# Log-sum-exp over rows on one core: rows split 112 plus 16 instead of 120 plus 8, a smaller final store, and the rarely used second pass placed in front of the first in the program

## Chip, core, metric

One core of a Trainium2 chip runs the kernel alone. The metric is device time in microseconds (us), the median of several executions. The profile's span leaves out some 1.8 us that the time has besides (163.79 against 162.0 in the profiled run of before).

## The reference

```python
x = randn(32, 512, 1024)                        # float32, 67.1 MB
max_x = max(x, axis=-1)
out = max_x + log(sum(exp(x - max_x), axis=-1)) # 16384 results
```

## The kernel before

The 16384 rows lie on 128 partitions, 128 rows each. The first pass does without the maximum: it takes Exp, sums, and Ln, and counts whether any sum is out of range. Only if one is, a second pass, with the maximum, overwrites the result. For inputs like these it never runs, but its code is in the program.

Rows come in 17 groups through a ring of 48 rows per partition. `R5` is one Exp of 5 rows on ScalarE and one reduction on VectorE; `T3` is an Exp and then for each row a half-add with accumulation on VectorE; `A` is one row that ScalarE both exponentiates and sums. Each load goes out on SyncE's queue and leaves sixteen updates of its semaphore in the records; those of the last load came from 157.57 to 158.13 us, and the Exp that needs it started at 158.16.

```python
B = 8; W = NC - B                  # NC = 128 rows per partition
x_rows = x_flat[0 : P * W].rearrange("(p c) d -> p c d", p=P)
x_rest = x_flat[P * W : n].rearrange("(p c) d -> p c d", p=P)
loads = ["R8 R8", "R8 R8", "R8 R8", "R7 R6 A A", "R6 R5 A A A", "R5 R4 A", "R5 R4", "R5 T3",
         "R3 A A A", "R3 A", "R2 T2", "R3", "R1 A", "T2", "T1", "A", "A"]
REST = 7; EARLY = 104; LATE = 118
for i, ops in enumerate(loads):    # the eighth group comes from x_rest, columns 0 to 7
    ...                            # load, Exp, sums
    if following == EARLY + 14:
        nc.scalar.activation(out=res[:, 0:EARLY], in_=sumexp[:, 0:EARLY], func=AF.Ln)
    if following == LATE + 3:
        check(0, LATE, 0)          # range check of the sums on VectorE
nc.at_finalize(start_early)        # SyncE's first load goes to the top, before the opening barrier
nc.scalar.activation(out=res[:, EARLY:NC], in_=sumexp[:, EARLY:NC], func=AF.Ln)
nc.sync.dma_start(out=out_rest, in_=res[:, 0:B])     # 32 bytes a partition
nc.sync.dma_start(out=out_rows, in_=res[:, B:NC])    # 480 bytes a partition, the last to land
... # range check of the rest, flag to ScalarE and VectorE
with tc.If(all_fine < 1, preferred_fallthrough_block=False):
    ... # second pass, in steps of 48 rows
```

The order in which instructions stand on an engine is not the source's: a scheduler in the build decides it. In this kernel the source has the early Ln after the eleventh group (118 rows); in the trace below it ran at 141.67 us, in front of the Exps of groups ten and eleven.

Of the kernel before, what the change touches and what calls it, by code (L numbers as in the profile page):

```python
# [14 lines left out]
def kernel(  # L15
# [5 lines left out]
    nc = tc.nc  # L21
# [3 lines left out]
    AF = mybir.ActivationFunctionType  # L25
# [6 lines left out]
    NC = n // P  # L32
# [2 lines left out]



    B = 8
    W = NC - B
    x_rows = x_flat[0 : P * W].rearrange("(p c) d -> p c d", p=P)  # L40
    x_rest = x_flat[P * W : n].rearrange("(p c) d -> p c d", p=P)
    out_flat = out.rearrange("a b -> (a b)")
    out_rows = out_flat[0 : P * W].rearrange("(p c) -> p c", p=P)
    out_rest = out_flat[P * W : n].rearrange("(p c) -> p c", p=P)
# [3 lines left out]

    RING = 48
    loads = [  # L50
        "R8 R8", "R8 R8", "R8 R8", "R7 R6 A A", "R6 R5 A A A", "R5 R4 A", "R5 R4", "R5 T3",
        "R3 A A A", "R3 A", "R2 T2", "R3", "R1 A", "T2", "T1", "A", "A",
    ]
    loads = [[(op[0], int(op[1:] or 1)) for op in load.split()] for load in loads]
    assert sum(s for ops in loads for _, s in ops) == NC
    ENGINES = [mybir.EngineType.Activation, mybir.EngineType.DVE]
    REST = 7
    EARLY = 104
    LATE = 118
    LAST = NC - 1  # L60

    big = ctx.enter_context(tc.tile_pool(name="big", bufs=1))
# [3 lines left out]
    ring = big.tile([P, RING, d], fp32, name="ring")  # L66
    sumexp = stats.tile([P, NC], fp32, name="sumexp")
    res = stats.tile([P, NC], fp32, name="res")
# [10 lines left out]
    nc.vector.memset(far, 100 * HIGH)  # L79

    def source(c0, size):
        assert c0 >= B or (c0 == 0 and size == B)
        return x_rows[:, c0 - B : c0 - B + size, :] if c0 >= B else x_rest

    def load(p0, c0, size, i):


        step = {2: 4, 3: 2, 4: 2}.get(i, 1)
        return [
            nc.sync.dma_start(  # L90
                out=ring[k::step, p0 : p0 + size, :], in_=source(c0, size)[k::step]
            ).ins
            for k in range(step)
        ]
# [14 lines left out]
        )  # L109
        nc.tensor.matmul(count, lhsT=bad[:, i : i + 1], rhs=far, start=i == 0, stop=False)  # L110

    following = B
    p = 0
    for i, ops in enumerate(loads):
        size = sum(s for _, s in ops)
        if p + size > RING:
            p = 0
        if i == REST:
            c = 0
        else:  # L120
            c = following
            following += size
        dmas = load(p, c, size, i)
        if i == 0:
            first_load = dmas[0]
        for how, s in ops:
            v = ring[:, p : p + s, :]
            sums = sumexp[:, c : c + s]
            if how == "A":
                o = v if c < LAST else last_exp  # L130
                exp = nc.scalar.activation(out=o, in_=v, func=AF.Exp, accum_out=sums)  # L131
            else:
                exp = nc.scalar.activation(out=v, in_=v, func=AF.Exp)  # L133
            without_wait(exp, "loads", "the slot's earlier users came before this load")
            without_wait(exp, "exps", "the slot's earlier users came before this load")
            without_wait(exp, "sums", "the slot's earlier users came before this load")
            tc.add_to_no_dep_group("exps", exp.ins)
            added = []
            if how == "R":
                added = [nc.vector.reduce_sum(out=sums, in_=v, axis=AX.X)]  # L140
            elif how == "T":
                for r in range(s):
                    lo = ring[:, p + r, 0:H]
                    added.append(
                        nc.vector.scalar_tensor_tensor(  # L145
                            out=lo, in0=lo, scalar=1.0, in1=ring[:, p + r, H:d],
                            op0=ALU.mult, op1=ALU.add, accum_out=sums[:, r : r + 1],
                        )
                    )
            for add in added:  # L150
                for dma in dmas:
                    tc.declare_no_dep(add.ins, dma, reason="ScalarE has waited for it")
                without_wait(add, "loads", "they came before this one")
            for add in added:
                tc.add_to_no_dep_group("sums", add.ins)
            c += s
            p += s
            last_row = v
        for dma in dmas:
            tc.add_to_no_dep_group("loads", dma)  # L160
        if following == EARLY + 14:
            nc.scalar.activation(out=res[:, 0:EARLY], in_=sumexp[:, 0:EARLY], func=AF.Ln)  # L162
        if following == LATE + 3:
            check(0, LATE, 0)

    def start_early(program):

        blocks = program.main_func.blocks
        here = next(b for b in blocks if any(i.name == first_load.name for i in b.instructions))
        k = next(k for k, i in enumerate(here.instructions) if i.name == first_load.name)  # L170
        assert not here.instructions[k].has_wait()
        first = here.instructions.pop(k)
        top = blocks[0].instructions
        k = next(
            k for k, i in enumerate(top)
            if i.engine == mybir.EngineType.SP and isinstance(i, mybir.InstDrain)
        )
        top.insert(k, first)

    nc.at_finalize(start_early)  # L180

    nc.scalar.activation(out=res[:, EARLY:NC], in_=sumexp[:, EARLY:NC], func=AF.Ln)  # L182
    nc.sync.dma_start(out=out_rest, in_=res[:, 0:B])
    nc.sync.dma_start(out=out_rows, in_=res[:, B:NC])



    check(LATE, LAST, 1)
    nc.vector.reduce_max(out=bad[:, 3:4], in_=last_row[:, 0, 0 : d // 16], axis=AX.X)  # L189
    nc.vector.tensor_scalar(  # L190
        out=bad[:, 2:3], in0=bad[:, 3:4], scalar1=LOG_LOW, scalar2=None, op0=ALU.is_lt
    )
    nc.tensor.matmul(count, lhsT=bad[:, 2:3], rhs=far, start=False, stop=False)  # L193
    nc.tensor.matmul(count, lhsT=sumexp[:, LAST:NC], rhs=ones, start=False, stop=True)  # L194
    nc.vector.tensor_scalar(out=fine, in0=count, scalar1=HIGH, scalar2=None, op0=ALU.is_lt)  # L195
# [4 lines left out]
    with tc.If(all_fine < 1, preferred_fallthrough_block=False):  # L200
        with tc.tile_critical(sync_engine=mybir.EngineType.Activation):
            with nc.semaphore("landed") as landed, nc.semaphore("ready") as ready:
                rows = 0
                steps = 0
                for c0 in range(0, NC, RING):
                    s = min(RING, NC - c0)
                    v = ring[:, 0:s, :]
                    neg = clamped[:, c0 : c0 + s]
                    if c0:
                        nc.scalar.wait_ge(ready, steps)  # L210
                    for c1, s1 in ((0, B), (B, s - B)) if c0 == 0 else ((c0, s),):
                        nc.scalar.dma_start(
                            out=ring[:, c1 - c0 : c1 - c0 + s1, :], in_=source(c1, s1)
                        ).then_inc(landed, 16)
                        rows += 16
                    nc.vector.wait_ge(landed, rows)
                    nc.vector.tensor_reduce(
                        out=neg, in_=v, op=ALU.max, axis=AX.X, negate=True
                    ).then_inc(ready, 1)
                    nc.vector.wait_ge(ready, steps + 1)  # L220
                    nc.vector.tensor_add(
                        out=v, in0=v, in1=neg[:, :, None].to_broadcast([P, s, d])
                    ).then_inc(ready, 1)
                    nc.scalar.wait_ge(ready, steps + 2)
                    nc.scalar.activation(out=v, in_=v, func=AF.Exp).then_inc(ready, 1)
                    nc.vector.wait_ge(ready, steps + 3)
                    nc.vector.reduce_sum(
                        out=sumexp[:, c0 : c0 + s], in_=v, axis=AX.X
                    ).then_inc(ready, 1)
                    steps += 4  # L230
                nc.scalar.wait_ge(ready, steps)
                nc.scalar.activation(out=res, in_=sumexp, func=AF.Ln).then_inc(ready, 1)
                nc.vector.wait_ge(ready, steps + 1)
                nc.vector.tensor_sub(out=res, in0=res, in1=clamped).then_inc(ready, 1)
                nc.scalar.wait_ge(ready, steps + 2)
                nc.scalar.dma_start(out=out_rest, in_=res[:, 0:B]).then_inc(landed, 16)
                nc.scalar.dma_start(out=out_rows, in_=res[:, B:NC]).then_inc(landed, 16)
                nc.scalar.wait_ge(landed, rows + 32)


# [28 lines left out]
```

## Time and profile before

| | before |
|---|---|
| time, median | 163.84 us (163.82 to 163.94) |
| loads, first packet to last | 1.02 to 157.69 us, 428 GB/s |
| last row landed / its Exp starts | 158.13 / 158.16 us |
| early Ln: ScalarE reaches it / its sums are ready | 141.67 / 140.41 us |
| final store, issue to landing | 159.58 to 161.16 us |

The page gives busy shares, the windows view what moved in a stretch, the timeline when each instruction ran, with its idle time in brackets where there was some. The lines that carry these readings are in the prediction. Here is the timeline of ScalarE in the kernel before, around the Ln and up to the end (start, length, engine, line, what):

```profile
141.58 0.19 ACT L131 ACTIVATION_READ_ACCUMULATOR ring<-ring 128x1 f32 x1
141.67 0.27 ACT L162 ACTIVATE res<-sumexp 128x104 f32<-128x104 f32 x1
141.85 2.75 ACT L133 ACTIVATE ring<-ring 128x3072 f32<-128x3072 f32 x1
...
154.35 2.86 ACT L133 ACTIVATE ring<-ring 128x2048 f32<-128x2048 f32 x2 [0.24 <-DMA ring<-in_x_dram]
```

The Ln has no bracket: it ran at once. The only idle time behind it that the view reports is 0.24 us before the Exp at 154.35. ScalarE has almost no room in its last 17 us.

### The profile page before, as it was taken

What the parts mean: (1) busy time and instruction counts of PE and PEld (TensorE: products, weight loads), DVE (VectorE), ACT (ScalarE), POOL (GpSimd) and SP (SyncE); (2) the same over time, 40 slices, a digit from 0 to 9 for tenths busy, and PEclk for the clock granted to TensorE, in tenths of its full rate; (3) what the DMA queues carried; (4) which work ended last, traced back from release to release, by engine and by line L of the source; (5) the groups of instructions that cost most, each with busy time, mean ns of one, the idle gap of its engine ahead of it and who ended that gap; (6) DMA issues with size and microseconds to landing.
All of it is one profiled execution on the core that took longest, in us unless ns stands there. A gap on an engine that the chain in (4) does not pass through costs nothing.

```text
span 162.0 us, 216 instructions
## 1 busy us (share of the span) xinstructions
PE 0.6 (0%) x8; PEld 0.3 (0%) x8; DVE 122.4 (76%) x47; ACT 116.8 (72%) x53; POOL 0.2 (0%) x4
## 2 busy tenths in 40 slices
PE   0000000000000000000000000000000000000001
PEld 0000000000000000000000000000000000000000
DVE  0000000899949999499999995999998999979993
ACT  3000059980799609994599839999969599999993
POOL 0000000000000000000000000000000000000000
DMA  8995995996996999799999899899999999999980
GB/s 275 502 518 259 518 518 259 518 518 275 502 518 291 485 502 425 303 485 485 453 453 453 382 394 425 384 453 437 437 396 469 394 455 401 425 423 417 414 350 19
DMA packets 2818, 67.19 MB, mean 415 GB/s; under 512 B 640, under 2 KB 640, under 8 KB 1024
## 3 DMA queue, kind: packets, MB, share of 16 engines
q1 hardware_dynamic: 2816, 67.18, 97.0%
q14 instruction: 2, 0.02, 0.0%
HBM read 67.11 MB, written 0.07 MB: 415 GB/s over the span
## 4 chain that ended last, share of the span: by engine, by line
DMA 63%; DVE 22%; ACT 12%; issue 0%; SPq 0%; PE 0%; DVEq 0%; ACTq 0%
DMA ring<-in_x_dram 63%; DVE sumexp L140 21%; ACT ring L133 12%; DVE ring L145 1%; SPq L90 0%; PE count L193 0%; DVE clamped L102 0%; DVE bad L190 0%; DVE bad L189 0%; DVE clamped L106 0%; DVE fine L195 0%; PE count L194 0%; DVEq L102 0%; ACTq L133 0%
## 5 line engine op out<-in xcount | busy, mean ns | idle before, releaser
L140 DVE TENSOR_REDUCE sumexp<-ring 128x8 f32<-128x8192 f32 (+7 forms) x20 | 116.2, 5854 | 36.0 <-ACT ring L133 36.0
L133 ACT ACTIVATE ring<-ring 128x8192 f32<-128x8192 f32 (+7 forms) x24 | 101.7, 4283 | 42.0 <-DMA ring<-in_x_dram 41.9
L131 ACT ACTIVATE ring<-ring 128x1024 f32<-128x1024 f32 x12 | 12.5, 1040 | 0.0
L145 DVE SCALAR_TENSOR_TENSOR ring<-ring 128x512 f32<-128x512 f32 x8 | 5.1, 683 | 0.0
L131 ACT ACTIVATION_READ_ACCUMULATOR ring<-ring 128x1 f32 x12 | 2.2, 186 | 0.0
L77 ACT ACT_TABLE_LOAD x1 | 1.3, 1283 | 0.8 <-PEq L253 0.8
L131 ACT ACTIVATE last_exp<-ring 128x1024 f32<-128x1024 f32 x1 | 1.0, 1028 | 0.0
L110 PE MATMUL count<-far,bad 128*1 128x1 f32 x4 | 0.4, 164 | 158.8 <-DVE clamped L106 158.8
L78 DVE MEMSET ones<- 128x1 f32 x1 | 0.1, 59 | 0.9 <-PEq L253 0.9
L145 DVE DVE_READ_ACCUMULATOR ring<-ring 128x1 f32 x8 | 0.6, 81 | 0.0
L102 DVE TENSOR_SCALAR clamped<-sumexp 128x118 f32<-128x118 f32 (+1 forms) x2 | 0.4, 198 | 0.1
L106 DVE SCALAR_TENSOR_TENSOR clamped<-clamped,sumexp 128x118 f32<-128x118 f32 (+1 forms) x2 | 0.4, 224 | 0.1
L110 PEld LDWEIGHTS count<-far,bad 128*1 128x1 f32 x4 | 0.2, 80 | 158.9 <-DVE clamped L106 158.9
L195 DVE TENSOR_SCALAR fine<-count 1x1 int32<-1x1 f32 x1 | 0.1, 145 | 0.3 <-PE count L194 0.3
L162 ACT ACTIVATE res<-sumexp 128x104 f32<-128x104 f32 x1 | 0.3, 272 | 0.0
L182 ACT ACTIVATE res<-sumexp 128x24 f32<-128x24 f32 x1 | 0.2, 222 | 0.0
L189 DVE TENSOR_REDUCE bad<-ring 128x1 f32<-128x64 f32 x1 | 0.2, 219 | 0.0
L193 PE MATMUL count<-far,bad 128*1 128x1 f32 x2 | 0.2, 164 | 0.2 <-DVE bad L190 0.2
L194 PE MATMUL count<-ones,sumexp 128*1 128x1 f32 x2 | 0.2, 163 | 0.0
L131 ACT ACTIVATION_READ_ACCUMULATOR last_exp<-ring 128x1 f32 x1 | 0.2, 186 | 0.0
L190 DVE TENSOR_SCALAR bad<-bad 128x1 f32<-128x1 f32 x1 | 0.2, 153 | 0.0
L106 DVE DVE_READ_ACCUMULATOR clamped<-clamped,sumexp 128x1 f32 x2 | 0.2, 82 | 0.0
(7 smaller groups left out, 0.6 us busy)
## 6 DMA issues: line engine op xcount, KB each, us to landing
ring<-in_x_dram SPq DMA_DIRECT2D x2, 3840.0 KB, 27.7
ring<-in_x_dram SPq DMA_DIRECT2D x2, 3584.0 KB, 25.6
ring<-in_x_dram SPq DMA_DIRECT2D x1, 5120.0 KB, 31.3
ring<-in_x_dram SPq DMA_DIRECT2D x1, 4608.0 KB, 33.7
ring<-in_x_dram SPq DMA_DIRECT2D x1, 4096.0 KB, 29.3
ring<-in_x_dram SPq DMA_DIRECT2D x2, 2048.0 KB, 32.7
ring<-in_x_dram SPq DMA_DIRECT2D x1, 3072.0 KB, 36.2
ring<-in_x_dram SPq DMA_DIRECT2D x2, 1024.0 KB, 38.7
```

The costliest lines, as they stand in the source:

```text
L77: nc.scalar.preload_act_table_set("natural_log_exp_and_others")
L102: nc.vector.tensor_scalar(out=clamped[:, c0:c1], in0=sumexp[:, c0:c1], scalar1=LOW, scalar2=HIGH, op0=ALU.max, op1=ALU.min,)
L106: nc.vector.scalar_tensor_tensor(out=clamped[:, c0:c1], in0=clamped[:, c0:c1], scalar=0.0, in1=sumexp[:, c0:c1], op0=ALU.bypass, op1=ALU.n ...
L110: nc.tensor.matmul(count, lhsT=bad[:, i : i + 1], rhs=far, start=i == 0, stop=False)
L131: exp = nc.scalar.activation(out=o, in_=v, func=AF.Exp, accum_out=sums)
L133: exp = nc.scalar.activation(out=v, in_=v, func=AF.Exp)
L140: added = [nc.vector.reduce_sum(out=sums, in_=v, axis=AX.X)]
L145: nc.vector.scalar_tensor_tensor(out=lo, in0=lo, scalar=1.0, in1=ring[:, p + r, H:d], op0=ALU.mult, op1=ALU.add, accum_out=sums[:, r : r + 1],
L162: nc.scalar.activation(out=res[:, 0:EARLY], in_=sumexp[:, 0:EARLY], func=AF.Ln)
L182: nc.scalar.activation(out=res[:, EARLY:NC], in_=sumexp[:, EARLY:NC], func=AF.Ln)
L189: nc.vector.reduce_max(out=bad[:, 3:4], in_=last_row[:, 0, 0 : d // 16], axis=AX.X)
L190: nc.vector.tensor_scalar(out=bad[:, 2:3], in0=bad[:, 3:4], scalar1=LOG_LOW, scalar2=None, op0=ALU.is_lt)
```

## The change

The intent, as the diff tells: let the last store carry little (64 bytes a partition instead of 480), put the large one among the loads, and take the jump over the second pass out of the end of the program, where it costs (gaps of 0.36 us on ScalarE and 0.52 us on VectorE), to the very top, where both have little to do anyway (in the kernel before the first Exp starts at 22.04 us, the first reduction at 29.10). The early Ln stays after 118 rows in the source, but takes 112 columns instead of 104.

```diff
-    B = 8
+    B = 16
     loads = [
-        "R8 R8", "R8 R8", "R8 R8", "R7 R6 A A", "R6 R5 A A A", "R5 R4 A", "R5 R4", "R5 T3",
-        "R3 A A A", "R3 A", "R2 T2", "R3", "R1 A", "T2", "T1", "A", "A",
+        "R8 R8", "R8 R8", "R6 R5 R5", "R8 R8", "R6 R5 A A A A", "R4 R4 R4", "R7 A A", "R4 T3",
+        "R4 A", "T2 A", "R2 A", "T2 A", "T2", "T2", "T1", "A", "A",
     ]
-        if following == EARLY + 14:
-            nc.scalar.activation(out=res[:, 0:EARLY], in_=sumexp[:, 0:EARLY], func=AF.Ln)
-        if following == LATE + 3:
+        if c == LATE:
+            nc.scalar.activation(out=res[:, 0:W], in_=sumexp[:, 0:W], func=AF.Ln)
             check(0, LATE, 0)
 ...
+        barrier = [...]                     # the opening barrier of ScalarE and VectorE
+        here.instructions[0:0] = barrier    # now behind their jump
+        for b in [b for b in blocks if "_true" in b.name or "critical" in b.name]:
+            blocks.remove(b)
+            blocks.insert(blocks.index(here), b)    # second pass in front of the first
 ...
-    nc.scalar.activation(out=res[:, EARLY:NC], in_=sumexp[:, EARLY:NC], func=AF.Ln)
-    nc.sync.dma_start(out=out_rest, in_=res[:, 0:B])
-    nc.sync.dma_start(out=out_rows, in_=res[:, B:NC])
+    nc.scalar.activation(out=res[:, W:NC], in_=sumexp[:, W:NC], func=AF.Ln)
+    nc.sync.dma_start(out=out_rows, in_=res[:, 0:W])
+    nc.sync.dma_start(out=out_rest, in_=res[:, W:NC])
 ...
-                for c0 in range(0, NC, RING):
+                for c0 in range(0, NC, STEP):       # STEP = 6: a longer second pass
```

More of the change, by code (lines that the diff above doesn't have):

```diff
@@ L56 @@
     ENGINES = [mybir.EngineType.Activation, mybir.EngineType.DVE]
-    REST = 7
-    EARLY = 104
     LATE = 118
+    STEP = 6
     LAST = NC - 1
@@ L81, in source @@
     def source(c0, size):
-        assert c0 >= B or (c0 == 0 and size == B)
-        return x_rows[:, c0 - B : c0 - B + size, :] if c0 >= B else x_rest
+        assert c0 >= W or c0 + size <= W
+        return x_rest[:, c0 - W : c0 - W + size, :] if c0 >= W else x_rows[:, c0 : c0 + size, :]
     def load(p0, c0, size, i):
@@ L110, in check @@
         nc.tensor.matmul(count, lhsT=bad[:, i : i + 1], rhs=far, start=i == 0, stop=False)
-    following = B
+    c = 0
     p = 0
@@ L117 @@
             p = 0
-        if i == REST:
-            c = 0
-        else:
-            c = following
-            following += size
         dmas = load(p, c, size, i)
@@ L160, with arrange @@
             tc.add_to_no_dep_group("loads", dma)
-        if following == EARLY + 14:
-            nc.scalar.activation(out=res[:, 0:EARLY], in_=sumexp[:, 0:EARLY], func=AF.Ln)
-        if following == LATE + 3:
+        if c == LATE:
+            nc.scalar.activation(out=res[:, 0:W], in_=sumexp[:, 0:W], func=AF.Ln)
             check(0, LATE, 0)
-    def start_early(program):
+    def arrange(program):
         blocks = program.main_func.blocks
+        top = blocks[0].instructions
         here = next(b for b in blocks if any(i.name == first_load.name for i in b.instructions))
@@ L172, in start_early @@
         first = here.instructions.pop(k)
-        top = blocks[0].instructions
         k = next(
@@ L178, in start_early @@
         top.insert(k, first)
-    nc.at_finalize(start_early)
-    nc.scalar.activation(out=res[:, EARLY:NC], in_=sumexp[:, EARLY:NC], func=AF.Ln)
-    nc.sync.dma_start(out=out_rest, in_=res[:, 0:B])
-    nc.sync.dma_start(out=out_rows, in_=res[:, B:NC])
+        barrier = [
+            i for i in top
+            if i.engine in ENGINES and isinstance(i, (mybir.InstDrain, mybir.InstEventSemaphore))
+        ]
+        assert len(barrier) == 2 * len(ENGINES)
+        for i in barrier:
+            top.remove(i)
+        here.instructions[0:0] = barrier
+        for b in [b for b in blocks if "_true" in b.name or "critical" in b.name]:
+            blocks.remove(b)
+            blocks.insert(blocks.index(here), b)
+    nc.at_finalize(arrange)
+    nc.scalar.activation(out=res[:, W:NC], in_=sumexp[:, W:NC], func=AF.Ln)
+    nc.sync.dma_start(out=out_rows, in_=res[:, 0:W])
+    nc.sync.dma_start(out=out_rest, in_=res[:, W:NC])
     check(LATE, LAST, 1)
@@ L204 @@
                 steps = 0
-                for c0 in range(0, NC, RING):
-                    s = min(RING, NC - c0)
+                for c0 in range(0, NC, STEP):
+                    s = min(STEP, NC - c0)
                     v = ring[:, 0:s, :]
@@ L210 @@
                         nc.scalar.wait_ge(ready, steps)
-                    for c1, s1 in ((0, B), (B, s - B)) if c0 == 0 else ((c0, s),):
+                    edge = max(c0, min(W, c0 + s))
+                    for c1, c2 in ((c0, edge), (edge, c0 + s)):
+                        if c1 == c2:
+                            continue
                         nc.scalar.dma_start(
-                            out=ring[:, c1 - c0 : c1 - c0 + s1, :], in_=source(c1, s1)
+                            out=ring[:, c1 - c0 : c2 - c0, :], in_=source(c1, c2 - c1)
                         ).then_inc(landed, 16)
@@ L235 @@
                 nc.scalar.wait_ge(ready, steps + 2)
-                nc.scalar.dma_start(out=out_rest, in_=res[:, 0:B]).then_inc(landed, 16)
-                nc.scalar.dma_start(out=out_rows, in_=res[:, B:NC]).then_inc(landed, 16)
+                nc.scalar.dma_start(out=out_rest, in_=res[:, W:NC]).then_inc(landed, 16)
+                nc.scalar.dma_start(out=out_rows, in_=res[:, 0:W]).then_inc(landed, 16)
                 nc.scalar.wait_ge(landed, rows + 32)
```

## The prediction

> **What bounds the kernel now.** I read the page first: the busy line, then the slices, then the DMA queues.
>
> ```profile
> PE 0.6 (0%) x8; PEld 0.3 (0%) x8; DVE 122.4 (76%) x47; ACT 116.8 (72%) x53; POOL 0.2 (0%) x4
> ...
> q1 hardware_dynamic: 2816, 67.18, 97.0%
> q14 instruction: 2, 0.02, 0.0%
> HBM read 67.11 MB, written 0.07 MB: 415 GB/s over the span
> ```
>
> No compute engine is above 76%, while the load queue alone fills 97.0% of the time of 16 DMA engines. Next, the windows view of the load stretch and of the tail; its last two columns are the DMA share and GB/s.
>
> ```profile
> 1.00:158.00 157.00, 0.19 (x2) 0.09 (x2) 121.00 (x38) 115.02 (x49) 0.00 (x0) 1.00 1.00 427
> 158.00:162.00 4.00, 0.43 (x6) 0.22 (x6) 1.27 (x8) 1.53 (x5) 0.00 (x0) 1.00 0.07 19
> ```
>
> So the time has three pieces: 1.0 us until the first packet (packet records: 1.02 us), a stream without a gap from there to 157.69 us (67.11 MB in 156.67 us, 428 GB/s), and a tail of 4.3 us. After the span of 162.0 come 1.8 us more, since that run took 163.79. Only three things can save time: an earlier start, fewer bytes or less packet overhead, a shorter tail.
>
> The tail, in the timeline (start, length, engine, line):
>
> ```profile
> 157.11 1.04 ACT L131 ACTIVATE ring<-ring 128x1024 f32<-128x1024 f32 x1
> ...
> 158.16 1.03 ACT L131 ACTIVATE last_exp<-ring 128x1024 f32<-128x1024 f32 x1
> ...
> 159.12 0.19 ACT L131 ACTIVATION_READ_ACCUMULATOR last_exp<-ring 128x1 f32 x1
> ...
> 159.34 0.22 ACT L182 ACTIVATE res<-sumexp 128x24 f32<-128x24 f32 x1
> ...
> 159.58 0.34 SPq L184 DMA_DIRECT2D out_dram<-res  x1
> 159.64 0.14 DVE L195 TENSOR_SCALAR fine<-count 1x1 int32<-1x1 f32 x1 [0.33 <-PE count L194]
> ```
>
> The last row lands at 158.13 (its semaphore's sixteenth update), its Exp starts at 158.155, then accumulator, Ln, store at 159.58. The store's packets run from 160.42 to 160.77 and it lands at 161.16. Meanwhile ScalarE and VectorE load the flag and branch over the second pass. Who is waited for at the end, from the queue's waits within 156 to 162 us:
>
> ```profile
> SPq L264 <- DVEq L200: 0.5, 1, 0.5
> SPq L264 <- DMA out_dram<-res: 0.3, 1, 0.3
> SPq L264 <- ACTq L200: 0.3, 1, 0.3
> ```
>
> The sequencers' records give the order of arrival at the closing barrier: ScalarE's drain ends at 161.06, VectorE's at 161.25, SyncE's second drain (after the store landed) at 161.31, and the gather passes at 161.33. So SyncE and the store set the end, but VectorE is only 0.05 us behind as a second path. Its branch is slow: the jump's record starts at 160.63 and lasts 0.05, and the next record, the drain, starts at 161.20, a gap of 0.52 us. ScalarE has a gap of 0.36 us after its compare (160.37 to 160.73). [...] The two packets of the instruction queue, 8192 bytes each, start at 161.39 and 161.79, about 0.95 us after each of these gaps opens[...].
>
> [...]
>
> **The change part by part.**
>
> *Load list.* Still 17 groups and 128 rows per partition, and 22 load DMAs in the same partition splits. Between landings I read 19.345 us for 16 rows in one group and about 1.277 for one row: 15 rows are 18.07, so a row costs 1.2045 and a group some 0.07 beyond. 128 rows and 17 groups in both kernels: zero. Does the queue run dry? I stepped both lists through ring, engines and queue group by group, with the durations of this trace (Exp 0.85 us a row, reduction 1.08, half-add row 0.61). For before, this gives issues within 0.8 us of those traced (46.4, 65.8, 76.6, 85.2 us). For after, the tightest point is the group of nine rows: it must wait for the second reduction of the fourth group, about 104 us, and the queue still has some 7 us of bytes. No gap.
>
> *Tail of the load list.* The last rows arrive in groups of 2, 1, 1, 1 as before. The row sums put into half-adds (12 instead of 8 rows) and one row less on the accumulating Exp move VectorE's end of row sums from 158.47 to about 158.1, but ScalarE's last Exp waits for the last landing (158.13) anyway: zero on the path.
>
> *Stores.* The large one (now 112 columns, 448 bytes a partition) goes out after group eleven, about 147 to 149 us. It stands behind every load in the queue, as the old 32-byte one did (its packets ran 157.12 to 157.74), so it delays no load and lands by about 158.5, long before the end. The final one shrinks from 480 to 64 bytes a partition. Packets of 480 bytes took 26.4 ns, 32-byte ones 9.0; eight a DMA engine are 0.21 us; at an estimated 10 ns they are 0.08. Saved: 0.13. The Ln before it has 16 instead of 24 columns: from 104 columns (272 ns) against 24 (222) 0.6 ns a column, 0.005. The store path gets about 0.14 us shorter[...].
>
> *Code placement.* The jump at the very top costs VectorE and ScalarE perhaps half a microsecond there, and the opening barrier, which now comes after it, waits. SyncE's first load is issued before the barrier and fills the queue for 19 us, and the first Exp starts at 22.04: free. At the end the second pass is no longer in the way: [...]VectorE's drain comes at about 160.75 instead of 161.20. Alone that saves nothing, because the store lands later. Together with the small store it keeps VectorE from taking over: the store alone would gain only 0.05. The smaller steps of the second pass only make skipped code longer[...].
>
> *Sum.* 163.84 - 0.13 - 0.005 = about 163.70 us; span 162.0 to about 161.86.
>
> **The rivals.** (a) *Fetch among the loads.* The two 8192-byte fetches now probably happen near 1 us, among the first load packets. A fetch packet took 0.31 to 0.57 us on one DMA engine; every load needs all sixteen, and the last Exp starts only 0.02 us after the last landing, so a delay of the slowest engine goes straight to the end. The last load's sixteen updates spread from 157.57 to 158.13, so an early engine can absorb 0.3. For: nothing else hides. Against: only the latest few of 16 are exposed. It would make 163.75 to 164.0. (b) *Fetch or branch was the real end*: if the store's landing and VectorE's branch both fall and the postlude after the span also got its instructions late, up to 0.4 us goes: 163.4. For: a gap of 0.2 us in the closing semaphore steps at 162.3. Against: no fetch is seen there. [...] (d) *Starved queue* by the longer early groups: each microsecond of dry queue is a microsecond at the end; the 7 us in hand speak against it.
>
> **Range and chances.** Three runs before span 0.12 us. I take 163.70; (b) sets the lower end at 163.45, (a) the upper at 163.95. 2% would be 3.3 us, almost the whole tail: faster 0.01, same 0.98, slower 0.01 (only a dry queue could).
>
> **What would show it.** Right: the load stretch stays at 427 to 428 GB/s and ends within 0.1 us of 157.69; the last Exp starts near 158.15; the final store's packets take about 0.2 us instead of 0.35 and it lands 1.4 to 1.5 us after issue; VectorE's wait at the end line is gone from the queue's waits or ends before the store; the instruction packets lie near 1 us instead of 161. Wrong: a last landing later than 158.25 (rival a), idle DMA slices between 100 and 115 us (d), an unchanged landing time of the final store (c), or more than 0.3 us gone with the store saving only 0.14 (b).

The sum came to 163.70 us. Cut is what no trace of this case shows: one paragraph; what was thought to start the fetches at the end; a reading of 0.06 us for a jump at the top, and with it the size to which the two gaps at the end were to shrink; and rival (c), by which the small store gains nothing (163.84). That the stream could not run faster than its 428 GB/s was not shown: the sum takes the rate of the trace as it is.

## The result

The changed kernel took 165.50 us (165.40 to 165.59, 5 runs) against 163.86 us (163.82 to 164.12, 5 runs). The ratio is 1.0097, with a 95% interval of 1.0083 to 1.0111. Here and below a ratio is the mean time of one kernel's fast runs over that of the other's of the same rounds, so not quite the ratio of the medians. The kernel became 1.6 us slower, where 0.14 us had been forecast as gain.

The page of the changed kernel, busy line and queues, then its windows view of the load stretch and the tail (last two columns: DMA share, GB/s):

```profile
PE 0.7 (0%) x8; PEld 0.3 (0%) x8; DVE 121.6 (74%) x53; ACT 116.4 (71%) x51; POOL 0.2 (0%) x4
...
q1 hardware_dynamic: 2816, 67.18, 95.9%
q14 instruction: 2, 0.02, 0.0%
```

```profile
1.00:158.00 157.00, 0.19 (x2) 0.09 (x2) 118.86 (x41) 112.93 (x45) 0.00 (x0) 1.00 1.00 428
158.00:164.00 6.00, 0.55 (x6) 0.26 (x6) 2.79 (x12) 3.39 (x7) 0.00 (x0) 1.00 0.02 2
```

The load stretch is as full as before: no dry queue. But 2.1 us less of ScalarE's and of VectorE's work was done within it (ACT 112.93 against 115.02, DVE 118.86 against 121.00): the engines reach the end with more still to do. The timeline says since when. ScalarE in the changed kernel, with the last line from the whole timeline:

```profile
146.13 0.19 ACT L125 ACTIVATION_READ_ACCUMULATOR ring<-ring 128x1 f32 x1
148.57 0.30 ACT L156 ACTIVATE res<-sumexp 128x112 f32<-128x112 f32 x1 [2.25 <-DVE sumexp L134]
148.77 1.89 ACT L127 ACTIVATE ring<-ring 128x2048 f32<-128x2048 f32 x1
...
160.04 1.00 ACT L125 ACTIVATE last_exp<-ring 128x1024 f32<-128x1024 f32 x1
...
161.20 0.22 ACT L188 ACTIVATE res<-sumexp 128x16 f32<-128x16 f32 x1
...
161.44 0.34 SPq L190 DMA_DIRECT2D out_dram<-res  x1
```

And VectorE in the changed kernel, the reduction that the Ln waited for:

```profile
144.06 4.41 DVE L134 TENSOR_REDUCE sumexp<-ring 128x4 f32<-128x4096 f32 x1
```

The early Ln now reads columns 0 to 111. Columns 107 to 110 are summed by the reduction that starts at 144.06 and is over by 148.5; column 111 is an `A` row, summed by ScalarE itself before. The scheduler put the Ln in ScalarE's order in front of the Exps of the eleventh group (groups counted from one), so ScalarE stood idle for 2.25 us with loaded rows waiting (those of group eleven had landed at 146.13). From 148.57 on it runs without a reported gap, and its last Exp starts at 160.04, 1.44 us after the last row has landed (158.60).

A second thing is in the semaphore records. The last landing itself is 0.47 us later (158.60 against 158.13). Of the sixteen updates of each load, fourteen come within some 0.5 us, but the last two come some 0.47 and 0.63 us behind the fourteenth, in every load from the first (22.48 us) to the last. The two packets of the instruction queue, 8192 bytes each, which lay at 161.39 and 161.79 us, now start at 4.07 and 4.37 us, among the first loads.

At the very end, the waits of SyncE's queue from 156 us on:

```profile
SPq L273 <- DVEq L206: 0.4, 1, 0.4
SPq L273 <- DMA out_dram<-res: 0.4, 1, 0.4
```

The two lines look alike; which came last is in the sequencers' records: VectorE's drain (the last thing it does before the closing barrier) now ends at 162.48, long before SyncE's second drain at 163.01, which waited for the store. The store took 1.42 us from issue to landing instead of 1.58.

The sum in the span: the last Exp starts 1.88 us later (0.47 by its landing, 1.42 more by ScalarE, with rounding), the store lands 0.155 us faster behind its issue, the steps between gain 0.02: 1.7 us, as 163.7 against 162.0.

### The profile page after: what moved, and what is told of

It reads as the page before. It is cut to its first block, busy times and chain, and to the rows that moved or that the text cites. A ratio compares the mean times of both kernels' runs of the same rounds, so it can differ in the third digit from the quotient of the medians.

```text
span 163.7 us, 222 instructions
## 1 busy us (share of the span) xinstructions
PE 0.7 (0%) x8; PEld 0.3 (0%) x8; DVE 121.6 (74%) x53; ACT 116.4 (71%) x51; POOL 0.2 (0%) x4
## 4 chain that ended last, share of the span: by engine, by line
DMA 46%; DVE 33%; ACT 18%; issue 2%; SPq 0%; PE 0%; DVEq 0%; ACTq 0%
DMA ring<-in_x_dram 46%; DVE sumexp L134 30%; ACT ring L127 17%; DVE ring L139 2%; ACT ring L125 1%; SPq L89 0%; ACT res L156 0%; DVE bad L195 0%; PE count L199 0%; DVE clamped L101 0%; PE count L200 0%; DVE bad L196 0%; DVE fine L201 0%; DVE clamped L105 0%; DVEq L195 0%
## 5 line engine op out<-in xcount | busy, mean ns | idle before, releaser
L134 DVE TENSOR_REDUCE sumexp<-ring 128x8 f32<-128x8192 f32 (+5 forms) x18 | 112.7, 6310 | 36.1 <-ACT ring L127 36.1
L125 ACT ACTIVATE ring<-ring 128x1024 f32<-128x1024 f32 x11 | 11.4, 1041 | 0.0
L139 DVE SCALAR_TENSOR_TENSOR ring<-ring 128x512 f32<-128x512 f32 x12 | 7.7, 686 | 2.0 <-ACT ring L127 2.0
```

Source lines behind the costliest of these rows:

```text
L125: exp = nc.scalar.activation(out=o, in_=v, func=AF.Exp, accum_out=sums)
L134: added = [nc.vector.reduce_sum(out=sums, in_=v, axis=AX.X)]
L139: nc.vector.scalar_tensor_tensor(out=lo, in0=lo, scalar=1.0, in1=ring[:, p + r, H:d], op0=ALU.mult, op1=ALU.add, accum_out=sums[:, r : r + 1],
```

## The experiments

My theory (A) was that two independent losses had been bought: the wait in front of the Ln, and two instruction fetches that hold up DMA engines among the loads. The rivals were the load list itself with its busier VectorE (B), the fetches alone (C), fetches that cost nothing because ScalarE bounds the end (D), and the jump at the top with its later barrier and later second load (E). In the expectations of e1 and e6 groups are counted from one, in that of e5 from zero.

All seven kernels gave correct results. What the records of the nine profiled runs show, in us; "spread" is from the first to the sixteenth update of a load, for the first load and the last:

| run | time, median | 8192-byte fetches at | spread, first and last load | last landing | last Exp starts | final store, issue to landing |
|---|---|---|---|---|---|---|
| before | 163.86 | 161.39, 161.79 | 0.54, 0.56 | 158.13 | 158.16 | 1.58 |
| changed | 165.50 | 4.07, 4.37 | 1.13, 1.10 | 158.60 | 160.04 | 1.42 |
| e1 | 164.16 | 4.14, 4.29 | 1.27, 1.25 | 158.68 | 158.71 | 1.42 |
| e2 | 164.85 | 162.83, 162.89 | 0.79, 0.61 | 158.12 | 159.51 | 1.41 |
| e3 | 163.58 | 161.36, 161.43 | 0.41, 0.46 | 158.00 | 158.02 | 1.40 |
| e4 | 164.48 | 4.40, 4.54 | 1.28, 1.26 | 158.93 | 158.98 | 1.58 |
| e5 | 165.59 | 163.26, 163.65 | 0.68, 0.66 | 158.13 | 159.68 | 1.59 |
| e6 | 164.10 | 104.66, 155.64 | 0.64, 1.16 | 158.66 | 158.68 | 1.41 |
| e7 | 164.01 | 6.62, 161.90 | 1.14, 1.08 | 158.55 | 158.58 | 1.41 |

The kernel before had medians of 163.82 us beside e1 to e4 and 163.85 us beside e5 to e7 (9 runs each).

### e1: the Ln behind the next Exps

```diff
-            nc.scalar.activation(out=res[:, 0:W], in_=sumexp[:, 0:W], func=AF.Ln)
+            ln = nc.scalar.activation(out=res[:, 0:W], in_=sumexp[:, 0:W], func=AF.Ln)
+            tc.keep_in_program_order(ln)
```

> The changed kernel with one edit: the early Ln (112 columns) is pinned behind the Exps of group eleven (118 rows so far) on ScalarE, where the changed kernel's scheduler put it in front of them and it waited 2.2 us for VectorE. Theory A (the stall in front of the Ln is most of the loss, the two instruction fetches among the loads the rest): no wait at the Ln, the last Exp starts at the last landing, about 158.6, in place of 160.04; time about 164.1 us. Rival B (the load list itself, more half-adds and a busier VectorE, is the cause): 165.3 to 165.5. Rival C (the fetches are the whole cause): 165.5.

164.16 us (163.98 to 164.31), ratio to before 1.0016 (1.0002 to 1.0030). ScalarE's timeline of this run:

```profile
149.16 0.28 ACT L156 ACTIVATE res<-sumexp 128x112 f32<-128x112 f32 x1
...
154.91 2.86 ACT L127 ACTIVATE ring<-ring 128x2048 f32<-128x2048 f32 x2 [0.23 <-DMA ring<-in_x_dram]
...
158.71 1.02 ACT L125 ACTIVATE last_exp<-ring 128x1024 f32<-128x1024 f32 x1
```

The same Ln with the same columns now has no bracket; 0.6 us later in the stream its sums are there. The last Exp again starts right behind its landing (158.68), and 1.34 us of the time is back. The load list is unchanged here, so rival B falls, and so does C: the fetches are still in place and only a part of the loss is left.

### e2: the code placement undone

The second pass is behind the first again, in steps of 48 rows, and the barrier is at the top:

```diff
-    STEP = 6
+    STEP = RING
...
-        barrier = [...]
-        ...
-        for b in [b for b in blocks if "_true" in b.name or "critical" in b.name]:
-            blocks.remove(b)
-            blocks.insert(blocks.index(here), b)
```

> The changed kernel with the code of the second pass back behind the first one's, in steps of 48 rows, and the barrier back at the top; load list, stores and the place of the Ln as changed. Theory A: no instruction packet among the loads, the spread of a load's sixteen updates back from 1.13 to about 0.56 us, last landing about 158.13, but the Ln still waits some 2 us; VectorE's sums come some 0.5 us earlier with their landings, so about 165.0 us. Rival C (the fetches are the whole cause): 163.8. Rival D (ScalarE is the bound from the Ln on, the fetches cost nothing): 165.5.

164.85 us (164.74 to 165.06), ratio to before 1.0059 (1.0045 to 1.0073): 0.65 us less than the changed kernel. The last landing is back at 158.12. The waits view still has the Ln's wait:

```profile
ACT res L156 <- DVE sumexp L134: 2.2, 1, 2.2
```

Rival D falls too. ScalarE bounds the end in both kernels, yet taking the fetches away helps: the sums that the Ln waits for are themselves made of rows that land earlier. The whole stretch moves (the last landing by 0.48 us, the last Exp by 0.53), the wait keeps its length (2.2 us in both).

### e3: both undone

The two edits together. What stays of the change is the load list, the 112 plus 16 rows and the small store.

> Both edits of the two runs before in one kernel: what is left of the change is the load list with 112 plus 16 rows and the small final store. Theory A: last landing about 158.13, last Exp at once behind it, final store landed some 0.15 us sooner than in the kernel before; about 163.72 us, or 163.8 if VectorE's branch ends the program instead of the store. Rival B (load list): still above 164.5.

163.58 us (163.56 to 163.71), ratio to before 0.9985 (0.9971 to 0.9998). This version beats both kernels, by 0.15% against the one before, which is just clear of the noise. It is better than the 163.72 to 163.8 that I expected: its last landing came at 158.00, and no edit explains these 0.13 us. The two edits gave 1.34 and 0.65 us alone and 1.92 us together (165.50 to 163.58), so they add up almost fully: two losses, not one. The waits of SyncE's queue show what ends this version:

```profile
SPq L263 <- DVEq L196: 0.8, 1, 0.8
```

The landing of the store is no longer in the list. By the records VectorE's drain ends at 161.09, SyncE's second drain at 161.04: the faster store has made VectorE's branch the last to arrive, as the prediction said of the store alone.

### e4: the code placement alone, in the kernel before

The changed kernel's `arrange` and its steps of 6 rows, put into the kernel before (its `source` helper was widened to parts of the rest for it).

> The kernel before with the code placement alone (second pass in front, in steps of 6 rows, the jump at the top, the barrier after it). Theory A: two 8192-byte instruction packets near 4 us, two DMA engines some 0.5 us behind from the first load to the last, last landing about 158.6, and as ScalarE is released by it the time grows by as much: about 164.3 us. Rival D (the fetches cost nothing on the path): 163.8 to 163.9, or 0.05 less by the shorter branch.

164.48 us (164.37 to 164.61), ratio 1.0034 (1.0021 to 1.0048). The placement costs the kernel before 0.66 us, more than I had expected, since its last landing came at 158.93. That it is later than in e1 (158.68), with the same two fetches and another load list, says that the size of this loss is not fixed.

### e5: the wait alone, in the kernel before

```diff
-    EARLY = 104
+    EARLY = 110
...
-        if following == EARLY + 14:
+        if following == EARLY + 8:
```

> The kernel before with one number changed: its early Ln covers 110 columns in place of 104, at the same place in ScalarE's order. Columns 104 to 109 hold the sums of group eight, whose reduction of three rows ended at 143.68 while ScalarE reaches the Ln at 141.67. Theory A: ScalarE waits 2.0 us at the Ln, has only some 0.3 us of idle time left after it (0.24 before 154.35), and the last Exp starts some 1.7 us late: about 165.5 us. Rival B (a wait of ScalarE there is absorbed, the list was the cause): 163.8 to 164.0.

165.59 us (165.39 to 165.72, 4 runs), ratio 1.0106 (1.0090 to 1.0121). Six more columns in one Ln of 0.3 us cost 1.74 us. ScalarE's timeline:

```profile
143.77 0.29 ACT L162 ACTIVATE res<-sumexp 128x110 f32<-128x110 f32 x1 [2.00 <-DVE sumexp L140]
...
147.66 7.29 ACT L133 ACTIVATE ring<-ring 128x2048 f32<-128x2048 f32 x4
...
159.68 1.00 ACT L131 ACTIVATE last_exp<-ring 128x1024 f32<-128x1024 f32 x1
```

Loads, landings and code are those of the kernel before; the last row landed at 158.13 as there. The wait of 2.00 us comes out at the last Exp as 1.53 us (159.68 against 158.16); the other 0.2 us are VectorE's branch, whose drain now ends last (163.13, against 162.91 for SyncE's). The same loss appears without anything else of the change.

### e6: the second pass in front, but short

```diff
-    STEP = 6          # against e1
+    STEP = RING
```

> As e1 (Ln pinned later, second pass in front), but the second pass in steps of 48 rows, so that ScalarE's first pass starts 38 and VectorE's 57 instructions nearer to the program's start. Theory A (each engine fetches 8192 bytes more when it passes a fixed place in its code, and the fetch holds up one DMA engine's loads): the two instruction packets no longer lie near 4 us but somewhere in the middle of the loads, ScalarE's first; the spread of the sixteen updates is 0.4 to 0.6 us before the first packet and grows behind it; last landing 158.3 to 158.7, time 163.9 to 164.2. Rival E (what hurts is the jump at the top, the later barrier and the later second load, not the fetch): spread and last landing as in e1 from the first load on. Rival F (a fetch hurts only in the crowd of first packets): 163.6.

The fixed place in an engine's code is part of the theory: the records give the times of the packets, not the engine whose code they carry.

164.10 us (163.96 to 164.15), ratio 1.0014 (1.0001 to 1.0028). The fetches moved to 104.66 and 155.64 us, and the spread follows them: 0.61 to 0.64 us in every load up to the one that landed at 98.15, 0.95 in the next (113.00), 0.89 before the second fetch, 1.12 in the load that landed at 157.41 and 1.16 in the last. The jump at the top is in this kernel too, and the first load landed at 21.97 us, within the 21.80 to 22.04 of the four kernels without an early fetch (before, e2, e3, e5); with a fetch at the start it was 22.44 to 22.81. So E falls as the cause, and F (only the crowd at the start is dangerous) as well. The load that landed at 113.00 was 0.49 us behind its like in e3 (112.51), after 0.16 before the fetch: 0.33 more, about the 0.31 us that the packet took.

### e7: one fetch without any of the change's placement

```diff
     nc.vector.memset(far, 100 * HIGH)          # against e3
+    pad = stats.tile([P, 70], fp32, name="pad")
+    for k in range(70):
+        nc.vector.memset(pad[:, k : k + 1], 0.0)
```

> As e3 (the fast one, second pass behind, barrier at the top), with 70 more tiny memsets of an unused tile on VectorE right after the start, where it idles until 29 us. They push VectorE, and only it, over the place in its code where it fetches 8192 bytes, in the first few us. Theory A: one instruction packet within 3 to 6 us, the spread of the sixteen updates grows by 0.3 us or more from the first load on, last landing 158.2 to 158.5, time 163.8 to 164.1. Rival E (jump, barrier or later second load are to blame): nothing of these is in this kernel, so 163.58 as e3.

164.01 us (163.89 to 164.07), ratio 1.0009 (0.9995 to 1.0023), and 0.43 us more than e3. The memsets run while VectorE is idle: its longest wait for ScalarE, the one before its first reduction, is 26.2 us, against 27.9 in e3. What they move is one of the two instruction fetches, from the end to 6.62 us; the first load landed at 22.44 instead of 21.80, the last at 158.55 instead of 158.00, a little past what I expected. e3 and e7 ran in different rounds on different chips; against the kernel before of the same rounds the medians put the cost at 0.40 us. That is about what this one fetch among the loads cost.

### What the packet records add

Why did one packet of 0.31 us put the first load of e7 back by 0.64 us, and its load in e6 by 0.33? The records do not name the DMA engine of a packet, but sixteen chains can be told apart, since a load packet starts within some 5 ns of the end of another (98% of them in the kernel before). I take each chain for one engine. In e6 one load packet ends at 104.660 us, the fetch runs from 104.657 to 104.966, and the next load packet of that chain starts only at 104.963. It takes 2.14 us; the fifteen beside it take 1.82 to 1.85. So one engine fetched, and lost 0.30 us by the fetch and 0.31 by a slower load packet behind it. Until then it had been 0.32 us ahead of the slowest engine, so 0.3 of the 0.6 us came out at the landing. In the changed kernel the two chains with a fetch lost 0.83 and 0.73 us (their next load packets took 2.95 and 2.84 us instead of 2.42), and they are the last two of the sixteen at the first landing.

In e7 the fetch's engine lost 0.83 us. But another engine had been 0.3 us behind the rest before the fetch, since the first packets. The last update but one comes at 22.07 us in the first load and at 158.19 in the last, the last at 22.44 and 158.55. So about 0.37 us of e7's later landing is the fetch's, and the rest is a lag that was there before it.

What stays open: why the load packet behind a fetch is slower, by 0.31 to 0.57 us (changed, e1, e4, e6, e7), and why the spread of the first load differs by up to 0.38 us between the four kernels without an early fetch (0.41 to 0.79). Nor was the small store run alone; that it saves 0.16 us is read from its issue and landing only, in all five runs of the 64-byte store besides the changed kernel (1.40 to 1.42) against the three with 480 bytes (1.58 to 1.59).

## Why the prediction was wrong

- **What bounds the kernel: right.** The stream was full in both kernels (427 to 428 GB/s, though it ended at 158.14 us instead of 157.69), and no compute engine was busier than before. But "bounded by the loads" was true of the kernel before with next to no room on ScalarE behind 141 us, and the prediction did not ask how much.
- **Load list: right.** Stepping through the groups said that the queue would not run dry, and the windows show 428 GB/s. e3 with this list is the fastest version.
- **Stores: this is the step that failed.** "The large one (now 112 columns, 448 bytes a partition) goes out after group eleven, about 147 to 149 us" looked only at what the store would do to the queue, not at what its Ln waits for. The Ln stands in front of group eleven's Exps on ScalarE, as it had stood in front of those of groups ten and eleven in the profile before, and it waits for the sums up to column 110, which are there at 148.5. ScalarE gets there at 146.3. The store did go out at 148.9, inside the range, but only because of that wait. The runs put this term at 1.34 us (e1), and at 1.74 us in the kernel before (e5), where the prediction has none. The gain of the final store was right: 0.155 us measured for 0.13 forecast.
- **Tail of the load list: wrong with it.** "ScalarE's last Exp waits for the last landing (158.13) anyway: zero on the path" held wherever the Ln did not wait (e1, e3, e4, e6, e7: the last Exp within 0.05 us of the landing); in the changed kernel the last Exp waited for ScalarE itself, by 1.44 us.
- **Code placement: right at the end, "free" at the top was wrong.** VectorE's drain did move out of the way, by 0.53 us before SyncE's. But the price was not the jump or the barrier; it was where the fetches went. Rival (a) named exactly this mechanism, with the last landing as its sign, and gave it 163.75 to 164.0. The sum left it out because an early engine could absorb 0.3 us; it was mis-sized, since an engine that fetches loses 0.6 to 0.9 us by the packet records. Measured, the placement costs 0.65 us in the changed kernel (e2), 0.66 in the kernel before (e4) and 0.58 between e1 and e3.
- **Readings: two were off.** One took 0.737 to 0.797 us at the top of the kernel before for a jump, but there is no branch record there. Where a jump does stand at the top, in the changed kernel, the gaps are 0.53 us on VectorE and 0.39 on ScalarE, which bears out "perhaps half a microsecond"; at the end of that kernel VectorE's drain starts 0.09 us after the record before it. And the packets at 161.39 and 161.79 us start 1.02 and 1.11 us after the gaps open, not 0.95. The prediction did not ask where the final store's 1.58 us lie: 0.84 before the first packet, and only 0.4 after the last.
- **Rivals (b), (c), (d): none of them.** Nothing was gained at the end beyond the store, the shorter packets did show in the landing, and no slice ran dry.

What a fetch costs, by the records: in all nine traces the fetches are packets of 8192 bytes on a queue of their own (q14 on the page), two from the span's start on. One among the loads took 0.31 to 0.32 us (changed, e6), and the load packet behind it on its chain 0.31 to 0.57 us more than its like: 0.6 to 0.9 us on its engine. On the time it was 0.40 to 0.43 us for one fetch (e7) and 0.52 to 0.66 us for two (e1 and e6 against e3; e4 against before). The lag did not shrink: in the changed kernel the slowest engine was 0.63 us behind the fourteenth in the first load and 0.63 us in the last. That is why two late engines were the whole load's delay there: 14 of 16 updates were in time, and no Exp of a last load started before the sixteenth.

## What to carry to other kernels

Before giving an engine an instruction that needs another engine's result, look up where it stands in the built order and when its last input is ready; here, on an engine without room, one short instruction that waited blocked every ready one behind it (0.3 us of Ln, 2.25 us of wait), and at a place one group of ready work later it did not wait at all (e1). Code that never runs still has a place, and here its place moved the fetches: from 161 us to 4 us with a long second pass in front (e4 against before), to 104.66 and 155.64 us with a short one (e6). In this kernel, bound by its loads, the quiet time for them was after the last load, not while an engine idles: the last landing came at 158.00 to 158.13 us in the four kernels that fetched only then (before, e2, e3, e5), at 158.55 to 158.93 in the other five. When two parts of a change work against each other, undo each alone and both together: here the sum of both (1.92 us) showed that one part was worth keeping.
